# A dilated 3x3 convolution: half of one image's store given to 80, 21, 21 and 6 partitions in turn

## The chip, the cores and the metric

The kernel runs on one core of one Trainium2 chip. A core has TensorE (PE, the matrix unit), VectorE (DVE), ScalarE (ACT), GpSimd (POOL) and SyncE (SP); here SP only issues transfers and waits for them. Transfers between the chip's main memory and the core's SBUF (128 partitions) are carried by 16 DMA engines, which all of the core's queues share. Matmuls write their sums to PSUM, and DVE and ACT bring them from there to SBUF.

The metric is the time of one execution on the device, in microseconds (us); lower is better. The kernel before takes 126.75 us (median of 3 runs, 126.32 to 127.67).

## What is computed

Sixteen images of 64 channels and 64 x 64 points are convolved with 128 filters of 3 x 3 taps. The dilation is 2, and the borders are padded with zeros, so the output has 128 channels of 64 x 64.

```python
batch, c_in, h, w, c_out, k, dilation = 16, 64, 64, 64, 128, 3, 2
...
x_pad = np.pad(x, ((0, 0), (0, 0), (pad, pad), (pad, pad)), mode='constant')
output[b, co] += weight[co, ci, kh, kw] * x_pad[b, ci, kh*dilation:kh*dilation+h, kw*dilation:kw*dilation+w]
```

All arrays are float32. The input has 16.8 MB, the weights 0.3 MB, the output 33.6 MB: an image of the output is 128 channels of 16 KB.

## The kernel before

**Tiling.** Images are worked on in pairs: `pb` runs from 0 to 7 (`NP` is 8, line 30), and the two images of a pair, `hb` 0 and 1, lie in the two halves of the 128 partitions, 64 input channels each. In the output, the 128 output channels are the 128 partitions, so that one partition holds one channel: 64 rows of the image, 16 KB. A pair's output is the tile `o{pb}` (line 191) with the shape 128 x 2 x 64 x 64; its pool `opool` has three buffers.

**Compute.** Each pair is done in four steps `u` (line 193) of 16 image rows. In each of them three groups of matmuls (`phase`, line 181) use the sums of image rows two apart, so that a sum that two output rows need is worked out once: ACT copies the common part from PSUM to `s32` (line 204), and DVE adds it to the two others and writes to `o` (line 209). POOL prepares the sums of input rows (`prepare`, line 135).

**Loads.** The first pair of images is loaded by SP (line 75), the other seven by POOL (`load`, line 78), which turns them to float16 on the way. The pairs 1 to 4 are loaded at the start and each later one two pairs ahead (line 196).

**Stores.** SP issues all of them, in program order, each when DVE has written the last rows that it needs. The pairs 0 to 4 (`pb < BOTH`, and `BOTH` is 5) go out as one transfer of 4 MB (line 221). From pair 5 on, each image goes out by itself (line 224), and in the last pair each image in two halves of 32 rows, after two of the four steps each (`step`, line 217). That gives 13 stores, five of 4 MB, four of 2 MB (images 10 to 13) and four of 1 MB. At its end SP waits until the last of them have landed (shown with line 255).

The order of the work is the program's order: the schedule is manual (line 57), and what waits for what follows from the tiles that are read and written.

The eleventh image is image 10, the first of pair 5 (`pb` 5, `hb` 0). Its store is the first that line 224 issues.

Of the kernel before, what the change touches and what calls it, by code (L numbers as in the profile page):

```python
# [10 lines left out]
def kernel(  # L11
# [7 lines left out]
    nc = tc.nc  # L19

    B, CI, H, W = x.shape
# [56 lines left out]
    def load(pb, cuts):  # L78
        x16[pb] = x16pool.tile([P, H, W], f16, tag="x16", name=f"x16_{pb}")
        for lo, hi in zip(cuts, cuts[1:]):  # L80
            nc.gpsimd.dma_start(out=x16[pb][:, lo:hi], in_=x_pair[pb, :, lo:hi])  # L81
# [18 lines left out]
    for name, a in (("w21", 2), ("w01", 0)):  # L100
        for u in range(2):
            eng = nc.vector if name == "w21" else nc.gpsimd
            eng.tensor_sub(  # L103
                out=w16[:, SLOT[name] * KW : (SLOT[name] + 1) * KW, u, :],
# [8 lines left out]
    for n, name in enumerate(("w1", "w21", "w0", "w01", "w2")):  # L113
        ps = cpool.tile([P, 2, NB], f32, tag="ps", name=f"wt{n}")
        k0 = SLOT[name] * KW
        for j in range(KW):
            nc.tensor.matmul(  # L117
                out=ps[:, 0, j * CO : (j + 1) * CO],
# [16 lines left out]
    def prepare(pb, lo, hi):  # L135
        if pb not in s16:
            s16[pb] = sumpool.tile([P, 2 * NQ, W], f16, tag="s16", name=f"s16_{pb}")
        src = (x16[pb] if pb else x32).rearrange("p (q e r) w -> p q e (r w)", e=2, r=2)
        dst = s16[pb].rearrange("p (q r) w -> p q (r w)", r=2)
        q0, q1 = lo // 4, hi // 4  # L140
        nc.gpsimd.tensor_add(  # L141
            out=dst[:, q0:q1], in0=src[:, q0:q1, 0, :], in1=src[:, q0:q1, 1, :]
        )
# [37 lines left out]
    def phase(pb, u, terms):  # L181

        ps = cpool.tile([CO, 2, NB], f32, tag="ps", name="ps")
        for pair in zip(*(conv(pb, hb, ps[:, hb], u, terms) for hb in range(2))):
            for m in pair:
                nc.tensor.matmul(**m)  # L186
        return ps

    BOTH = NP - 3
    for pb in range(NP):  # L190
        o = opool.tile([P, 2, H, W], f32, tag="o", name=f"o{pb}")
        ov = o.rearrange("p b (q e r) w -> p b q e (r w)", e=2, r=2)
        for u in range(NU):

            if u == 1 and AHEAD <= pb + 2 < NP:
                load(pb + 2, [0, H])
            if pb + 1 < NP:
                if u == 1:
                    prepare(pb + 1, 0, 36)
                elif u == 2:  # L200
                    prepare(pb + 1, 36, H)

            s32 = spool.tile([P, 2, NB], f32, tag="s32", name="s32")
            nc.scalar.copy(out=s32, in_=phase(pb, u, [("w1", 2, 0)]))  # L204
            for e, terms in enumerate(
                ([("w21", 1, 0), ("w0", 1, -1)], [("w01", 0, 0), ("w2", 0, 1)])
            ):
                ps = phase(pb, u, terms)
                nc.vector.tensor_add(  # L209
                    out=ov[:, :, u * UQ : (u + 1) * UQ, e, :],  # L210
                    in0=ps.rearrange("p b (q c) -> p b q c", c=QW),
                    in1=s32.rearrange("p b (q c) -> p b q c", c=QW),
                )

            step = NU // 2 if pb == NP - 1 else NU
            if (u + 1) % step == 0:
                fl = slice((u + 1 - step) * 4 * UQ, (u + 1) * 4 * UQ)
                if pb < BOTH:  # L220
                    nc.sync.dma_start(out=out_pair[pb], in_=o)
                else:
                    for hb in range(2):
                        nc.sync.dma_start(out=out[2 * pb + hb, :, fl], in_=o[:, hb, fl])


# [33 lines left out]
```

## Time and profile before

| | |
|---|---|
| median of 3 runs | 126.75 us |
| span of the profiled execution | 124.3 us |
| PE busy | 105.2 us, 85% of the span |
| DVE busy | 80.8 us, 65% |
| ACT, POOL busy | 39.6 us, 41.4 us |
| moved by DMA | 43.4 MB, mean 349 GB/s; HBM read 17.07 MB, written 33.55 MB |
| stores of a pair (4 MB), median from issue to landing | 21.6 us |
| stores of an image (2 MB) | 12.4 us |
| stores of half an image (1 MB) | 10.6 us |

The span is one profiled execution, from its first to its last instruction. The time of a run is some 2.5 us longer, for what lies around the program. The profile cuts the span into 40 slices of 3.11 us and gives for each the busy share of every engine in tenths. A DMA share of 1 means that all 16 DMA engines carry packets.

Behind these tables lie the records of the single packets. A store of an image is 128 packets of 16 KB, one for each partition; each of the 16 DMA engines carries eight of them, one after the other, and then a packet of 4 bytes that reports its share as done. The store counts as landed when all 16 shares are reported. Each DMA engine works through its packets in the order of the stores.

### The profile page before, as it was taken

Reading aid. Unit: us, or ns where it says so; the run is one execution under the profiler, and the core shown is the slowest. Engines: PE = TensorE matmul, PEld = TensorE weight load, DVE = VectorE, ACT = ScalarE, POOL = GpSimd, SP = SyncE. Lnnn points to the kernel's source line nnn. Section 1 sums busy time; section 2 is a strip of 40 time slices with the busy share of each in tenths; the row PEclk is TensorE's granted clock in tenths of the full one; section 3 lists DMA queues with packets and bytes.
Section 4 is the critical chain, followed back from the end, with each engine's and each line's share of the span. In section 5 each row is a group of like instructions: output and inputs, shape, how many; then the busy total and the mean of one; then the engine's idle time right before and its main releaser. Section 6 shows DMA issues by size and latency. Waiting matters only on the chain.

```text
span 124.3 us, 2244 instructions
## 1 busy us (share of the span) xinstructions
PE 105.2 (85%) x981; PEld 55.7 (45%) x981; DVE 80.8 (65%) x71; ACT 39.6 (32%) x40; POOL 41.4 (33%) x33
## 2 busy tenths in 40 slices
PE   6357999999999999999999999999999999960000
PEld 2043555555555555555555555555555555520000
DVE  0470199787778777877769778777877787770000
ACT  4760823333333333333333333333332433320000
POOL 2859998794095009500930093000000000000000
PEclk9999999999999999999999999999999999999655
DMA  4999999999999999999999999999999999999991
GB/s 129 346 359 218 214 214 216 224 237 411 393 327 314 332 306 319 316 390 314 324 345 427 425 427 432 422 427 427 432 438 427 432 414 432 427 417 419 422 406 71
DMA packets 3961, 43.42 MB, mean 349 GB/s; under 512 B 368, under 2 KB 368, under 8 KB 624
## 3 DMA queue, kind: packets, MB, share of 16 engines
q1 hardware_dynamic: 2944, 35.95, 68.9%
q0 software_dynamic: 1008, 7.34, 28.4%
q8 instruction: 7, 0.11, 0.3%
q14 instruction: 2, 0.02, 0.0%
HBM read 17.07 MB, written 33.55 MB: 407 GB/s over the span
## 4 chain that ended last, share of the span: by engine, by line
PE 80%; DMA 5%; POOL 2%; DVE 1%; DVEq 1%; SPq 0%; issue 0%
PE ps L186 80%; DMA x<-in_x_dram 5%; POOL s L141 2%; DVE o L209 1%; DVEq L255 1%; SPq L64 0%; DVEq L209 0%
## 5 line engine op out<-in xcount | busy, mean ns | idle before, releaser
L209 DVE TENSOR_TENSOR o<-ps,s 128x1024 f32<-128x1024 f32 x64 | 76.7, 1223 | 25.9 <-PE ps L186 16.8
L186 PE MATMUL ps<-x,w_sb 64*128 64x496 f16 (+3 forms) x768 | 85.3, 368 | 0.0
L186 PEld LDWEIGHTS <-w_sb 64*128 64x128 f16 x960 | 53.4, 95 | 49.3 <-issue 3.7
L204 ACT COPY s<-ps 128x1024 f32<-128x1024 f32 x32 | 32.4, 1012 | 63.0 <-PE ps L186 63.0
L141 POOL TENSOR_TENSOR s<-x 128x1152 f16<-128x1152 f16 (+4 forms) x18 | 35.1, 1971 | 31.1 <-PE ps L186 28.3
L186 PE MATMUL ps<-s,w_sb 64*128 64x496 f16 (+1 forms) x192 | 26.5, 379 | 2.1 <-POOL s L141 2.1
L81 POOL DMA_DIRECT2D x<-in_x_dram x7 | 4.0, 579 | 0.0
L132 ACT CAST x<-x 128x1024 f16<-128x1024 f32 (+1 forms) x3 | 2.8, 973 | 3.4 <-DMA x<-in_x_dram 3.4
L93 PE MATMUL warm<-zero 128*128 128x512 f16 x6 | 2.7, 630 | 1.2 <-DVE zero L87 1.2
L117 PE MATMUL wt<-ident,w 128*128 128x128 f16 x15 | 1.8, 312 | 2.1 <-ACT w L99 2.1
L103 DVE TENSOR_TENSOR w<-w 128x192 f16<-128x192 f32 x2 | 1.5, 800 | 2.5 <-DMA w<-in_weight_dram 2.5
L117 PEld LDWEIGHTS <-w 128*128 128x128 f16 x15 | 1.5, 146 | 3.0 <-ACT w L99 3.0
L99 ACT CAST w<-w 128x576 f16<-128x576 f32 x2 | 2.3, 1222 | 1.6 <-DMA w<-in_weight_dram 1.6
L103 POOL TENSOR_TENSOR w<-w 128x192 f16<-128x192 f32 x2 | 1.9, 951 | 2.4 <-DMA w<-in_weight_dram 2.4
L126 DVE CAST w_sb<-wt 128x384 f16<-128x384 f32 x3 | 1.6, 552 | 1.4 <-PE wt L117 1.4
L93 PEld LDWEIGHTS <-zero 128*128 128x128 f16 x6 | 0.7, 138 | 2.3 <-DVE zero L87 1.2
L99 ACT ACT_TABLE_LOAD x1 | 1.3, 1283 | 0.7 <-PEq L241 0.7
L128 ACT CAST w_sb<-wt 128x384 f16<-128x384 f32 x2 | 1.0, 478 | 1.1 <-PE wt L117 1.1
L130 DVE CAST x<-x 128x1280 f16<-128x1280 f32 x1 | 0.8, 826 | 0.5 <-DMA x<-in_x_dram 0.5
L87 DVE MEMSET zero<- 128x256 uint32 x1 | 0.3, 272 | 0.9 <-PEq L241 0.9
masks.py:199 POOL TENSOR_SCALAR_AFFINE_SELECT ident<-ident 128x128 f16<-128x128 f16 x1 | 0.3, 292 | 0.1
masks.py:197 POOL MEMSET ident<- 128x128 f16 x1 | 0.2, 204 | 0.3 <-POOLq L241 0.3
(4 smaller groups left out, 0.4 us busy)
## 6 DMA issues: line engine op xcount, KB each, us to landing
out_dram<-o SPq DMA_DIRECT2D x5, 4096.0 KB, 21.6
out_dram<-o SPq DMA_DIRECT2D x4, 2048.0 KB, 12.4
x<-in_x_dram POOLq DMA_DIRECT2D x7, 1024.0 KB, 16.0
out_dram<-o SPq DMA_DIRECT2D x4, 1024.0 KB, 10.6
x<-in_x_dram SPq DMA_DIRECT2D x1, 1152.0 KB, 6.5
x<-in_x_dram SPq DMA_DIRECT2D x1, 896.0 KB, 10.6
w<-in_weight_dram SPq DMA_DIRECT2D x1, 288.0 KB, 2.9
```

Of the source, the lines that this page charges most:

```text
L81: nc.gpsimd.dma_start(out=x16[pb][:, lo:hi], in_=x_pair[pb, :, lo:hi])
L93: nc.tensor.matmul(out=warm[:, 0], lhsT=zero[:, 0:P], rhs=zero, start=True, stop=True)
L99: nc.scalar.copy(out=w16[:, 0:NK, u, :], in_=w32k)
L103: eng.tensor_sub(out=w16[:, SLOT[name] * KW : (SLOT[name] + 1) * KW, u, :], in0=w32k[:, a * KW : (a + 1) * KW, :], in1=w32k[:, KW : 2 * KW ...
L117: nc.tensor.matmul(out=ps[:, 0, j * CO : (j + 1) * CO], lhsT=w16[:, k0 + j, :, :].rearrange("o t i -> o (t i)"), rhs=ident, start=True, st ...
L126: nc.vector.tensor_copy(out=dst, in_=ps[:, 0, 0 : KW * CO])
L132: nc.scalar.copy(out=x16[0][:, lo:hi], in_=x32[:, lo:hi])
L141: nc.gpsimd.tensor_add(out=dst[:, q0:q1], in0=src[:, q0:q1, 0, :], in1=src[:, q0:q1, 1, :])
L186: nc.tensor.matmul(**m)
L204: nc.scalar.copy(out=s32, in_=phase(pb, u, [("w1", 2, 0)]))
L209: nc.vector.tensor_add(out=ov[:, :, u * UQ : (u + 1) * UQ, e, :], in0=ps.rearrange("p b (q c) -> p b q c", c=QW), in1=s32.rearrange("p b ( ...
L255: with _tile.TileContext(nc) as tc:
```

## The change

Only the store of image 10 is changed (`UNEVEN` is 2 x `BOTH`, that is 10). Where one transfer carried its 64 rows from all 128 partitions, five now follow one another on SP. The first carries rows 0 to 31 from all 128 partitions, 8 KB from each. The other four carry rows 32 to 63, 8 KB from each partition as well: from partitions 0 to 79, 80 to 100, 101 to 121, and 122 to 127. Bytes, places and compute are as before, and so are all other stores, which are issued in the same order behind these.

```diff
     BOTH = NP - 3
+    UNEVEN = 2 * BOTH
+    GROUPS = (80, 21, 21, 6)
     for pb in range(NP):
...
                     for hb in range(2):
-                        nc.sync.dma_start(out=out[2 * pb + hb, :, fl], in_=o[:, hb, fl])
+                        b = 2 * pb + hb
+                        if b != UNEVEN:
+                            nc.sync.dma_start(out=out[b, :, fl], in_=o[:, hb, fl])
+                            continue
+                        half = H // 2
+                        nc.sync.dma_start(out=out[b, :, 0:half], in_=o[:, hb, 0:half])
+                        p0 = 0
+                        for n in GROUPS:
+                            nc.sync.dma_start(
+                                out=out[b, p0 : p0 + n, half:H],
+                                in_=o[p0 : p0 + n, hb, half:H],
+                            )
+                            p0 += n
```

## The prediction

> **What bounds the kernel now.** I read the page's slices first, then the chain of waits, then stretches of the tail, then the store issues.
>
> ```profile
> span 124.3 us, 2244 instructions
> ...
> PE   6357999999999999999999999999999999960000
> ...
> DMA  4999999999999999999999999999999999999991
> GB/s 129 346 359 218 214 214 216 224 237 411 393 327 314 332 306 319 316 390 314 324 345 427 425 427 432 422 427 427 432 438 427 432 414 432 427 417 419 422 406 71
> ```
>
> A slice is 3.11 us. TensorE ends in slice 36; the DMA engines stay full to slice 39. From slice 22 on, when the loads are done, they move 406 to 438 GB/s without a hole: stores queue up and are worked off at a fixed rate.
>
> ```profile
> 9.95 99.61 PE ps L186 x948
> ...
> 109.66 1.23 DVE o L209
> 110.88 1.13 DVEq L255
> ```
>
> In the chain of waits (start, us, what) the last compute ends at 110.9 us and the chain stops at 112.0, 12.3 us before the span does. What fills that is the store queue. SyncE's waits say so:
>
> ```profile
> SPq L255 <- DMA out_dram<-o: 9.2, 4, 2.4
> ```
>
> SP waits at the end (line 255) for four stores, up to 2.4 us each. So a microsecond in DMA is a microsecond at the end, and one in compute is none. The stretches of the tail (columns: us, the five engines' busy time, PEclk, DMA share, GB/s):
>
> ```profile
> 90.00:119.00 29.00, 20.66 (x200) 10.76 (x196) 17.04 (x15) 6.73 (x7) 0.00 (x0) 0.94 1.01 427
> ...
> 120.00:120.50 0.50, 0.00 (x0) 0.00 (x0) 0.00 (x0) 0.00 (x0) 0.00 (x0) 0.50 0.85 360
> ...
> 121.00:121.50 0.50, 0.00 (x0) 0.00 (x0) 0.00 (x0) 0.00 (x0) 0.00 (x0) 0.50 0.66 279
> 121.50:122.00 0.50, 0.00 (x0) 0.00 (x0) 0.00 (x0) 0.00 (x0) 0.00 (x0) 0.50 0.35 147
> 122.00:122.50 0.50, 0.00 (x0) 0.00 (x0) 0.00 (x0) 0.00 (x0) 0.00 (x0) 0.50 0.16 66
> 122.50:123.00 0.50, 0.00 (x0) 0.00 (x0) 0.00 (x0) 0.00 (x0) 0.00 (x0) 0.50 0.04 16
> ```
>
> The 16 DMA engines do not finish together: the share falls from full at 120 us to one engine at 122.5. The trace's packet records give each engine's end, as an engine starts its next packet 3 ns before the last one ends: 120.55, 120.56, 120.58, 120.72, 121.22, 121.37, 121.62, 121.76, 121.79, 121.90, 121.92, 122.08, 122.14, 122.38, 122.71 and 122.91 us. Mean 121.64. Behind the last come 0.47 us until it is reported (123.37) and 0.89 us of closing (124.26). The median 126.75 is 2.5 us above this span; I add differences to the median.
>
> Followed back, the unevenness is old. When the third pair store ended, eight engines were within 0.42 us of each other (71.76 to 72.17) and eight came 0.9 to 1.9 us behind the first (72.67 to 73.67). Two things moved engines between these groups later. A 16 KB instruction fetch (at 73.3, 86.7, 99.8 us) each time set one engine back by about 1.3 us. And one engine, from 67 us on, took some 640 ns for each 16 KB row where all others took 611; it was among the early eight and ends last, at 122.91. The records don't number engines, so which is which is not known.
>
> **The change part by part.** Removed: one transfer of 128 rows of 16 KB, 8 rows per engine, 8 x 0.608 = 4.86 us of each engine. Added: 128 rows of 8 KB in one transfer, and another 128 rows of 8 KB as 80, 21, 21 and 6.
>
> *Rows per engine.* An 8 KB row holds an engine for 306 ns (309 ns long, 3 ns overlap). Bytes don't change; who carries them does. Every transfer of before was cut into 16 equal shares of whole rows. The trace shows no transfer whose rows 16 doesn't divide; the bounds are 48 rows (21 + 21 + 6) spread over all, 3 each, which changes nothing, and all on one engine, 48 x 0.306 = 14.7 us. I take equal shares of whole rows on as many engines as that allows up to 16, nearest to what the trace has: 80 is 16 x 5, 21 is 7 x 3, 6 is 6 x 1. If the shares begin at the same engine each time, six engines carry 5+3+3+1 = 12 rows, one 11 and nine 5, in place of 8. So +4 x 0.306 = +1.22 us for six, +0.92 for one, -0.92 for nine. [...]
>
> *What that does to the end.* The backlog is unbroken from 87 us on, so an engine's end moves by its own change.
> - Best by these ends: the seven earliest get the rows. The sixth ends at 121.37 + 1.22 = 122.59, the last at 122.91 - 0.92 = 121.99: end -0.3 us.
> - Worst: the last engine gets them: +1.22 us.
> - Between: nine of sixteen are relieved, so I take the engine of 122.91 as relieved (121.99). Of the early eight it leaves seven, and if these carry the rows, the latest is 122.14 + 1.22 = 123.36: +0.45 us. I take this, since the early eight are the one group of the right size that the trace shows.
>
> *Small terms.* Two 8 KB rows hold an engine for 612 ns where one of 16 KB held it for 608: 8 x 4 = 0.03 us. Four more completion packets, 6 ns each, 0.02 us. Together +0.05, already late engines included, left out of the forecast and inside the range.
>
> *Four more issues on SP.*
>
> ```profile
> L224 SPq DMA_DIRECT2D out_dram<-o x8: 332/730/1371, 87.3 to 112.4; - x8
> ```
>
> Issue times are min/median/max ns. Five at 87.3 take 1.7 to 6.9 us, so the twelfth image's store, queued behind them on SP, goes out by 89.0 to 94.2 and takes up to 1.4 more, 95.6. The cover is the backlog: the first engine ends the previous pair store at 91.2 and has 13 rows of this image at least (8 + 5), to 95.2. So nothing, or at most 0.4 us on an early, relieved engine, which isn't the last. Without the backlog it would be 1.3 to 5.5 us. SP's next store is due at 99.7, and each store waits for the completion of an older one on a reused semaphore: shifted by four, the closest is the fifth pair store, landed by 93.9. No wait, and no compute instruction needs this tile again.
>
> Sum: 122.91 becomes 123.36, span 124.3 to 124.7, time 126.75 + 0.45 = 127.2 us.
>
> **The rivals.**
>
> *Partitions are shared (slower).* In the kernel before, each engine always reads its own eight rows of 128, so the 611 ns can be the engine's rate or that of the eight partitions it reads; min and median of 611 at every phase speak for neither. If the partitions set it, two engines on one group of eight halve each other. Partitions 0 to 79 then need 8 rows from each of ten groups, 2.45 us in place of 1.53: +0.92. The 48 rows from partition 80 up lie in groups whose own engines are at work on the next image, so 7 rows take twice their time: 7 x 0.306 = +2.14. A loaded engine gets +1.22 + 0.92 + 2.14 = +4.28; the one at 122.14 ends at 126.4, +3.5 us: 130.25. If the last engine is loaded, 131.0. From the best case without sharing (-0.92) the sign turns once sharing costs a loaded engine 0.9 us; from my forecast the time is past +1% from 0.8 us on. For it: engines at one fixed rate, whatever their lead. Against it: no row shows two engines on one group. [...]
>
> *The ends come together (a little faster).* If the loaded seven are those of the early half that no instruction fetch hits, they end at about 120.7 + 1.22 = 121.9, the other nine by 121.99: -0.92 us, 125.8. At the seven earliest ends of the trace it is -0.3, 126.45. For it: an early half exists from 72 us on, and seven is nearly its size. Against it: fetches and the slow engine had pulled four of the eight back by the end.
>
> *It does not shift anything.* The 48 rows are spread over all 16 engines: 126.8.
>
> **How the numbers follow.** 1% is 1.27 us, about what a measurement can tell from no change here. The end moving by engine, between +0.2 and +1.3 us (127.0 to 128.0): 0.38, forecast 127.2. Ends coming together, -0.92 to +0.2: 0.24. Shared partitions: 0.35, with prices from +1.3 up to +4.3 and beyond. No shift: 0.03. Faster by over 1% needs -1.27 us; even all sixteen ends at the mean of 121.64 would give just that: 0.02. Slower by over 1%: the shared partitions and 0.03 of the first case: 0.38. Within 1%: 0.60. The range goes from 125.8 (ends together) to 131.1 (sharing with the last engine loaded), which leaves out some 0.12 of the sharing case and 0.04 elsewhere.
>
> **What would show it.** Right: after about 91 us six engines carry 12 rows; rows stay at 309 and 611 ns; the fall of the DMA share begins near 120 us and ends near 123.4; PE, DVE and ACT are unchanged to 111 us. Sharing: rows of 8 KB at up to 600 ns between 93 and 101 us and a stretch there well under 427 GB/s. Ends together: the share falls from full to nothing within a microsecond, before 122.5 us. I am wrong outright if SP's issue time opens a hole in the DMA share near 95 us, or if the rows of 21 go to another number of engines than seven.

## The result and the profile after

The changed kernel takes 130.74 us (median of 6 runs, 129.91 to 131.9) against 126.57 us beside it: ratio 1.0325, 95% interval 1.0272 to 1.0377, so about 4.1 us slower. The longest run of each kernel, 131.9 and 128.3 us, is left out of the ratio. The time lies in the range, but not at the forecast of 127.2: what came is the rival in which engines share partitions, put at 130.25. The profiled execution took 131.68 us, so what it shows adds up to more than 4.1 us: its last store is reported 5.4 us later than before.

The page of the changed kernel, its slices now 3.25 us long:

```profile
span 129.9 us, 2249 instructions
...
DMA  5999999999999999999999999999999999999720
GB/s 148 351 344 212 217 217 212 219 315 424 348 313 313 328 325 341 363 328 303 333 419 441 419 424 444 424 424 439 396 383 275 386 424 424 421 416 421 303 111 23
```

The DMA row (busy share) is as full as before; the row below it (GB/s) isn't. In slices 29 to 32 the rate falls to 396, 383, 275 and 386 GB/s, and it tails off over the last three slices. Stretches of the kernel before (us, the engines' busy time, PEclk, DMA share, GB/s):

```profile
94.00:96.00 2.00, 2.00 (x23) 1.04 (x20) 1.89 (x2) 0.00 (x0) 0.00 (x0) 1.00 1.00 426
96.00:98.00 2.00, 2.00 (x24) 1.09 (x22) 1.18 (x2) 1.01 (x1) 0.00 (x0) 1.00 1.04 442
98.00:100.00 2.00, 2.00 (x24) 1.17 (x22) 1.72 (x2) 0.99 (x1) 0.00 (x0) 1.00 1.01 426
100.00:102.00 2.00, 2.00 (x24) 1.01 (x20) 1.87 (x2) 0.02 (x1) 0.00 (x0) 1.00 0.99 414
102.00:104.00 2.00, 2.00 (x22) 1.08 (x20) 1.25 (x2) 1.01 (x1) 0.00 (x0) 1.00 0.96 410
```

The same stretches of the changed kernel, and its end:

```profile
94.00:96.00 2.00, 2.00 (x22) 1.02 (x20) 1.58 (x2) 0.14 (x1) 0.00 (x0) 1.00 0.95 356
96.00:98.00 2.00, 2.00 (x23) 1.02 (x20) 1.19 (x2) 1.01 (x1) 0.00 (x0) 1.00 1.13 352
98.00:100.00 2.00, 2.00 (x24) 1.14 (x22) 2.00 (x2) 0.69 (x1) 0.00 (x0) 1.00 1.05 295
100.00:102.00 2.00, 2.00 (x24) 1.08 (x20) 1.57 (x3) 0.33 (x1) 0.00 (x0) 1.00 0.90 344
102.00:104.00 2.00, 2.00 (x24) 1.00 (x20) 1.25 (x2) 1.01 (x1) 0.00 (x0) 1.00 0.98 377
...
106.00:112.00 6.00, 4.97 (x50) 2.38 (x44) 4.51 (x5) 1.52 (x2) 0.00 (x0) 1.00 1.00 426
...
122.00:123.00 1.00, 0.00 (x0) 0.00 (x0) 0.00 (x0) 0.00 (x0) 0.00 (x0) 0.50 0.53 221
...
124.00:126.00 2.00, 0.00 (x0) 0.00 (x0) 0.00 (x0) 0.00 (x0) 0.00 (x0) 0.50 0.27 115
126.00:128.00 2.00, 0.00 (x0) 0.00 (x0) 0.00 (x0) 0.00 (x0) 0.00 (x0) 0.50 0.12 49
128.00:129.00 1.00, 0.00 (x0) 0.00 (x0) 0.00 (x0) 0.00 (x0) 0.00 (x0) 0.50 0.02 8
```

Two losses can be read. From 94 to 104 us, when image 10's last rows and image 11 go out, the engines are busy and move 295 to 377 GB/s where before they moved 410 to 442. Against 427 GB/s that is (71 + 75 + 132 + 83 + 50) x 2 us = 0.82 MB, or 1.9 us of all engines. And the ends spread: the share falls from about 121 to 128.4 us, where before it fell from 120 to 122.9. The 16 shares of the last store are reported between 121.12 and 128.77 us, the last one 4.8 us after the mean; before it was between 120.87 and 123.37, and 1.4. So the mean of the engines is 2.0 us later, which agrees with the 1.9 us of lost rate, and the spread adds 3.4.

The rows themselves are slow. In the records from 94 to 104 us, 25 of 146 rows of 8 KB took 600 ns or more, the longest 3.0 us; before, such a row took 309. SP's waits for the last four stores show both losses:

```profile
SPq L269 <- DMA out_dram<-o: 14.6, 4, 7.4
```

They add up to 14.6 us, where they were 9.2; the longest is 7.4 us, where it was 2.4. The four added issues are not the cause:

```profile
L234 SPq DMA_DIRECT2D out_dram<-o x4: 352/1030/1123, 87.6 to 90.2; - x4
```

They are out by 91.3 us, image 11 behind them by 92.6, and by the records the engines carry packets for 97% or more of each microsecond from 90 to 104 us. The run with the same parts in another order, below, has as many issues and takes 2.6 us less.

### The profile page after: what moved, and what is told of

Read it like the earlier page. It is cut to its first block, busy times and chain, and to the rows that moved or that the text cites. A ratio compares the mean times of both kernels' runs of the same rounds, so it can differ in the third digit from the quotient of the medians.

```text
span 129.9 us, 2249 instructions
## 1 busy us (share of the span) xinstructions
PE 105.6 (81%) x981; PEld 54.4 (42%) x981; DVE 81.1 (62%) x71; ACT 39.5 (30%) x40; POOL 41.4 (32%) x33
## 4 chain that ended last, share of the span: by engine, by line
PE 77%; DMA 4%; POOL 2%; DVE 1%; DVEq 1%; SPq 0%; issue 0%
PE ps L186 77%; DMA x<-in_x_dram 4%; POOL s L141 2%; DVE o L211 1%; DVEq L269 1%; SPq L64 0%; DVEq L211 0%
## 5 line engine op out<-in xcount | busy, mean ns | idle before, releaser
L186 PE MATMUL ps<-x,w_sb 64*128 64x496 f16 (+3 forms) x768 | 86.2, 371 | 0.0
L186 PEld LDWEIGHTS <-w_sb 64*128 64x128 f16 x960 | 52.8, 95 | 50.6 <-issue 4.3
L117 PE MATMUL wt<-ident,w 128*128 128x128 f16 x15 | 1.2, 219 | 2.2 <-ACT w L99 2.1
L117 PEld LDWEIGHTS <-w 128*128 128x128 f16 x15 | 0.9, 98 | 3.2 <-ACT w L99 3.0
```

What stands on the lines that cost most here:

```text
L117: nc.tensor.matmul(out=ps[:, 0, j * CO : (j + 1) * CO], lhsT=w16[:, k0 + j, :, :].rearrange("o t i -> o (t i)"), rhs=ident, start=True, st ...
```

## The experiments

Two theories were put against each other: the load of the engines (12, 11 and 5 rows) costs the time, or sharing does, that is, rows take longer when engines read certain partitions at the same time. All edits are to the branch for image 10, and give its last 32 rows, unless said otherwise. Ratios are to the kernel before, run on the same chip.

**Two halves without groups.**

```diff
-                        p0 = 0
-                        for n in GROUPS:
+                        PARTS = [slice(0, 128)]
+                        for ps_ in PARTS:
                             nc.sync.dma_start(
-                                out=out[b, p0 : p0 + n, half:H],
-                                in_=o[p0 : p0 + n, hb, half:H],
+                                out=out[b, ps_, half:H],
+                                in_=o[ps_, hb, half:H],
                             )
-                            p0 += n
```

The next five kernels differ from this one in `PARTS` alone.

> Image 10 in two transfers of 128 rows of 8 KB each, no groups. Sharing theory (two DMA engines that read the same group of eight partitions halve each other): every engine reads its own eight rows as before, so rows stay at 309 ns and the time at that of before, 126.6 us, ratio 0.995 to 1.005. Uneven-load theory (the +4.2 us come from 12, 11 and 5 rows per engine): 8 rows each, also 126.6 us. If the splitting of the image itself or the early issue of its first half costs something, it shows here, as more than +0.6 us.

127.16 us, ratio 1.0045 (1.0016 to 1.0075), +0.6 us. A little more than nothing, and below what was named as a sign. Rows are at 309 ns and the mean of the last store's reports is that of before (121.91 against 121.98 us), so the profile, which is of the shortest of ten executions (126.5 us), doesn't show where it goes. It stays open, and the following runs are read against it.

**80 and 48.**

```diff
+                        PARTS = [slice(0, 80), slice(80, 128)]
```

> The last 32 rows of image 10 by 80 and then 48 partitions: 5 + 3 = 8 rows on each of 16 engines, so the load is even, but engines no longer read their own eight partitions. Uneven-load theory: 126.6 us (0 +- 0.6). Sharing theory: the 80 take 8 row times in place of 5 (+0.92 us), the 48 take 6 in place of 3 (+0.92): +1.8 us, 128.4 us, with 8 KB rows of 0.6 us and more between 94 and 101 us, and more if the engines that were held up meet others on the next image.

128.18 us, 1.0139 (1.0068 to 1.0210). The load is even and the time still rises, by 1.2 us over the two halves (some 0.2 to 2.2 by the two intervals); the load alone doesn't explain that. Rows of up to 1.29 us are among its records.

**64 and 64, and 64 in the middle.**

```diff
+                        PARTS = [slice(0, 64), slice(64, 128)]
```

> The last 32 rows of image 10 by partitions 0 to 63 and then 64 to 127: four rows on each of 16 engines twice, even load. Uneven-load theory: 126.6 us. [...]

127.67 us, 1.0070 (1.0016 to 1.0123).

```diff
+                        PARTS = [slice(32, 96), slice(0, 32), slice(96, 128)]
```

> The last 32 rows of image 10 by partitions 32 to 95 (4 rows per engine), then 0 to 31 and 96 to 127 (2 rows each): even load, three transfers. [...] If groups are eight neighbouring partitions, the middle has 8 groups for 16 engines, and so 8 rows at 0.61: +2.45 us, 129.0 us. If the cost lay on the side of the main memory (64 neighbouring channels written at once), it would be as for 64 and 64. Uneven-load theory: 126.6 us.

126.95 us, 1.0050 (1.0015 to 1.0086). By groups of eight neighbours, as the prediction had them, sharing would cost +2.45 us in either (8 rows at 0.61 us in place of 0.31). They cost 0.3 and 0.1 us over the two halves, and by the intervals that can be nothing at all. The load theory's 126.6 fits as well as any. So the price was wrong, or the engines are not all at the same part at once: in the kernel before, the early ones were up to 1.9 us ahead at 72 us, and four rows take 1.2. The one profile of 64 and 64 is of its longest execution, 129.72 us, which the ratio leaves out, and there rows are held up: up to 1.38 us for 8 KB, and 352 to 401 GB/s from 96 to 102 us. No profile shows how the others escaped that. The next pairs of runs were meant to leave less room for engines out of step.

**28 partitions by seven engines.** The other 100 partitions' rows are left out.

```diff
+                        PARTS = [slice(0, 28, 4), slice(1, 28, 4), slice(2, 28, 4), slice(3, 28, 4)]
```

> Of the last 32 rows of image 10 only partitions 0 to 27 are stored (the other 100 are left out, 0.8 MB less), by four transfers of 7 partitions each: 0, 4, 8, ... 24; then 1, 5, ... 25; and so on. [...] Rows at 309 ns. Seven engines save 4 rows against before (-1.22 us), nine save 8 (-2.45 us), so 124.2 to 125.4 us.

The same 28 partitions, seven neighbours in each transfer:

```diff
+                        PARTS = [slice(0, 7), slice(7, 14), slice(14, 21), slice(21, 28)]
```

> [...] If the load of an engine is all that counts: as with the strided ones, 124.2 to 125.4 us, rows at 309 ns. [...]

125.57 us, 0.9909 (0.9876 to 0.9941), and 125.68 us, 0.9921 (0.9893 to 0.9948): no difference, and no verdict. Leaving out 0.8 MB had emptied the queue of some engines before image 12's store came at 99.6 us, as the strided one's stretches show in the DMA share:

```profile
98.00:99.00 1.00, 1.00 (x14) 0.57 (x10) 1.00 (x2) 0.11 (x1) 0.00 (x0) 1.00 1.03 442
99.00:100.00 1.00, 1.00 (x16) 0.61 (x12) 0.60 (x1) 0.91 (x1) 0.00 (x0) 1.00 0.87 352
100.00:101.00 1.00, 1.00 (x12) 0.53 (x10) 0.98 (x1) 0.00 (x0) 0.00 (x0) 1.00 0.80 328
```

The records hold four rows over 550 ns with neighbours and none with the stride: the direction fits sharing, but the times are 0.1 us apart.

**64 partitions alone.** Here the kernel before is the base, at line 224. Half of the rows of images 12 and 13 are left out.

```diff
-                        nc.sync.dma_start(out=out[2 * pb + hb, :, fl], in_=o[:, hb, fl])
+                        b = 2 * pb + hb
+                        ch = slice(0, 64) if b in (12, 13) else slice(0, P)
+                        nc.sync.dma_start(out=out[b, ch, fl], in_=o[ch, hb, fl])
```

> The kernel before with only partitions 0 to 63 of images 12 and 13 stored, one transfer each (the other halves are left out): 4 rows of 16 KB on each of 16 engines per image. Engine-rate theory: half the time for these two images, rows at 611 ns, -4.3 us (the last stores are issued at 112 us and take 4.9 us and 1.4 us to close): 122.3 us. Sharing theory: 64 partitions are 8 groups, rows of 1.22 us wherever all 16 engines are at them, and the two images take as long as before: 126.6 us. [...]

```diff
+                        ch = slice(32, 96) if b in (12, 13) else slice(0, P)
```

> As the run with partitions 0 to 63, but with partitions 32 to 95 of images 12 and 13 (the others are left out): the same bytes, engines and rows per engine. [...] Engine-rate theory: 122.3 us for both.

Partitions 0 to 63: 125.64 us, 0.9906 (0.9868 to 0.9945). Partitions 32 to 95: 121.47 us, 0.9600 (0.9552 to 0.9647). Same bytes, engines and rows for each, and 4.2 us apart. One stretch of either profile, 0 to 63 first:

```profile
104.00:108.00 4.00, 4.00 (x40) 2.13 (x38) 3.25 (x3) 1.01 (x1) 0.00 (x0) 1.00 1.04 229
```

```profile
104.00:108.00 4.00, 4.00 (x41) 2.15 (x39) 3.25 (x4) 1.01 (x1) 0.00 (x0) 1.00 0.93 395
```

The engines are busy in both (shares of 1.04 and 0.93), and one moves 229 GB/s, the other 395. In the records of the first, rows of 16 KB cluster near 1,268 ns, in the second at 611. So it counts which 64 partitions the engines read: with 0 to 63 a row takes about twice as long. (In the first profile the rate is still 393 GB/s from 101 to 102 us and 311 in the two microseconds behind: the loss builds up, which fits engines that start out of step.) Groups of eight neighbours would make both runs alike, and fall. The records name neither an engine's partitions nor its number, so which partitions hold each other up is not shown.

**Load and sharing taken apart.** Four kernels have the change's load and its rows of 8 KB to the same 128 places, so the places in the main memory can't explain a difference between them. Of the 80 rows and of the 48, each can be read from neighbouring partitions, as in the change, or from spread ones: the 80 from partitions 32 to 95 and once more from every fourth of them, the 48 from every fourth partition of 0 to 24, 32 to 56 and 33 to 53. The expectations call the spread ones "own groups" and the neighbours "foreign". No record shows which engine reads which partitions; what either choice does shows in the time and in the length of the rows. Where spread partitions are used, some are read twice or more and others not, so the values stored are others. Both from spread partitions (the first two transfers are the 80, the loop is the 48: four rows on seven engines, two on seven, one on six):

```diff
-                        p0 = 0
-                        for n in GROUPS:
+                        nc.sync.dma_start(out=out[b, 0:64, half:H], in_=o[32:96, hb, half:H])
+                        nc.sync.dma_start(out=out[b, 64:80, half:H], in_=o[32:96:4, hb, half:H])
+                        r32 = o.rearrange("p two (s h) w -> p (two s) (h w)", s=2)
+                        for p1, n, k, c0 in ((0, 7, 4, 80), (32, 7, 2, 108), (33, 6, 1, 122)):
                             nc.sync.dma_start(
-                                out=out[b, p0 : p0 + n, half:H],
-                                in_=o[p0 : p0 + n, hb, half:H],
+                                out=out[b, c0 : c0 + n * k, half:H].rearrange(
+                                    "(n k) h w -> n k (h w)", k=k
+                                ),
+                                in_=r32[p1 : p1 + 4 * n : 4, 0:k],
                             )
-                            p0 += n
```

> [...] Sharing theory: only the load is left, +0.3 to +1.2 us, and the 0.5 us that the two halves cost: 127.2 to 128.4 us, with all rows at 309 ns but those of the one slow engine.

The 80 from spread partitions, the 48 from neighbours:

> [...] Same load of engines. [...] Uneven-load theory: as the change, 130.7 us, and as the run with own groups.

The 80 from neighbours, the 48 from spread partitions:

> [...] Same load of engines. Sharing theory: +0.9 us over the run with own groups for the 80, 128 to 129.3 us, less than the run in which the 48 are foreign. Uneven-load theory: 130.7 us.

| 80 rows | 48 rows | median us | ratio (95%) | mean report | last after mean |
|---|---|---|---|---|---|
| spread | spread | 127.96 | 1.0121 (1.0088 to 1.0154) | +0.3 us | 2.4 us |
| neighbours | spread | 128.38 | 1.0130 (1.0068 to 1.0192) | +0.4 us | 2.9 us |
| spread | neighbours | 129.00 | 1.0187 (1.0122 to 1.0252) | +1.5 us | 2.8 us |
| neighbours | neighbours (the change) | 130.74 | 1.0325 (1.0272 to 1.0377) | +2.0 us | 4.8 us |

The last two columns are from one profile each: how much later than before the 16 shares of the last store are reported in the mean, and how far the last one comes after that (1.4 us before).

With both from spread partitions the rate holds from 94 to 100 us, where the change's fell, as its stretches show:

```profile
94.00:96.00 2.00, 2.00 (x22) 1.02 (x19) 1.25 (x2) 0.53 (x1) 0.00 (x0) 1.00 1.01 422
96.00:98.00 2.00, 2.00 (x22) 1.11 (x20) 1.23 (x2) 0.99 (x1) 0.00 (x0) 1.00 1.05 442
98.00:100.00 2.00, 2.00 (x24) 1.16 (x22) 1.94 (x2) 0.33 (x2) 0.00 (x0) 1.00 1.05 446
100.00:102.00 2.00, 2.00 (x24) 1.13 (x20) 1.59 (x2) 0.71 (x1) 0.00 (x0) 1.00 0.91 381
```

Rows of 8 KB take 356 ns at most there, in the change up to 3.0 us. From 100 to 102 us the rate falls with the DMA share: by the records, three engines run empty at 100.4 to 100.6 us and start again at 101.3 to 101.4, when image 12's store is there. The relief of these three was lost again.

The load theory wanted 130.7 us in all four and falls. Over the two halves' 1.0045 the load alone costs 0.76%, 1.0 us (some 0.4 to 1.5). Over spread partitions, neighbours for the 80 add 0.09%, which is not distinguishable from nothing; for the 48, 0.66%, 0.8 us, at the edge of what these runs can tell; for both, 2.04%, 2.6 us (some 1.8 to 3.4), which is clear. The two together seem to cost more than their sum of 0.9 us. That rows already late from the 80 run into the others' rows would explain it, but is argued only.

**The same parts in another order.**

```diff
-    GROUPS = (80, 21, 21, 6)
+    GROUPS = (21, 21, 6, 80)
```

> The change with the four parts in another order: 21, 21 and 6 from partitions 0 to 47, then 80 from partitions 48 to 127. Bytes, rows per engine (12, 11, 5) and number of transfers as in the change. Uneven-load theory: 130.7 us. [...]

128.05 us, 1.0118 (1.0076 to 1.0160): level with the spread partitions, and 2.6 us below the change, with the same part sizes and the same load. Its stretches:

```profile
96.00:98.00 2.00, 2.00 (x24) 1.05 (x22) 1.19 (x2) 1.01 (x1) 0.00 (x0) 1.00 1.05 389
98.00:100.00 2.00, 2.00 (x24) 1.21 (x22) 1.88 (x2) 0.81 (x1) 0.00 (x0) 1.00 1.03 410
```

Rows are still held up (to 1.06 us in the records, and the rate is below 427), but the last share is reported at 125.50 us, not at 128.77. So the price isn't one of the part sizes: it depends on which partitions each part has, or on when it goes out. Order and partitions changed together here, so the run doesn't say which of the two matters more.

No version was found that beats the kernel before.

## Why the prediction was right or wrong

- *The bound.* Right: compute ends at about 112 us in both profiles, and the difference is all in the store queue.
- *Rows per engine.* Right. The records of landings show 16 engines reporting for the 80, and 7, 7 and 6 for the others.
- *An engine's end moves by its own change.* This is the step that failed. It took each row at 306 ns whoever reads beside it, priced the load alone and left sharing to the rival. In the change rows of 8 KB took up to 3.0 us, and it takes 2.6 us more than the same load from spread partitions. What the load itself costs was within the bounds of -0.3 and +1.22: 1.0 us over the two halves, where +0.45 was taken.
- *The last engine is relieved.* Wrong, and with it the forecast of +0.45. In the changed kernel the engine with long rows (8 KB in 314 to 347 ns) shows 3, 3 and 1 of them behind its share of the 80: it is one of the six that carry 12. It is through with image 10 at 99.65 us, before at 98.43: 1.22 us later, as the worst case had it. That was the one to take for the load: with spread partitions the last report comes at 124.70 us, 1.3 us after that of before.
- *Sharing.* The rival held, with the wrong parts. Put at +0.92 for the 80 and +2.14 for the 48, together 3.1 us, it cost about 0.1, 0.8 and together 2.6 us. Full halving was assumed for every row, by groups of eight neighbours, which the two runs of 64 partitions alone contradict; which partitions hold each other up, no run shows; the runs with 64 and 64 cost nearly nothing, and that engines out of step escape sharing fits them but is argued. So it is partly luck that 130.25 lies near 130.74: sharing was put too high, the splitting's 0.6 us was left out, and the loaded engine was taken as one that ends 0.8 us before the last.
- *Small terms and issues.* The splitting was put at 0.05 us and cost 0.6 (0.2 to 0.95). The issues were covered, as said; but the first half left at 81.3 us, not at 87.3, since its rows are complete two steps earlier.
- *The chances.* Sharing had 0.35 and the load alone 0.38. The rate of 611 ns was taken to speak for neither, and so it was: only other partitions told the theories apart, with rows of 16 KB near 1,268 ns on 0 to 63 and at 611 on 32 to 95.

## What to carry to other kernels

In this kernel an engine's share of a store could not be moved, with the right values stored, without moving which partitions it reads. With the queue full, transfers of all 128 partitions kept rows of 8 KB at 309 ns; the cut into 80, 21, 21 and 6 gave that up, with rows of up to 3.0 us. To see it, read GB/s beside the DMA share: an engine whose row is held up counts as busy (a share of 1.04 at 229 GB/s with 64 partitions alone).

## What was not expected

- The delay is neither even nor bounded by two: an 8 KB row took up to 3.0 us, nearly ten times its 309 ns, while other rows beside it stayed at 309. What held it up, the records don't say.
- The same four part sizes in another order cost 2.6 us less (1.0118 against 1.0325).
- A cut into 64 and 64 costs next to nothing (1.0070 against 1.0045) where the same 64 partitions alone, for two images in a row, run at 229 GB/s.
